# Two feature tiles of the FFN side by side, token combinations on VectorE, and weight parts issued later

## The chip, the cores and the metric

The kernel runs on one core of one Trainium2 chip. The metric is the device time of one execution in microseconds (us). Before the change the median of three runs is 2619.1 us (2618.94 to 2619.82).

## The reference

The program is a decoder trunk of two layers over 1040 tokens (16 meta tokens and 1024 inputs), model width 1024, all in float32:

```python
for l in range(DEPTH):
    h = rms_norm(h_res, attn_norm_g[l])
    z = h @ w_in[l]
    c_q, c_kv, k_pe, rq, rk, rv, rg = jnp.split(z, split_idx, axis=-1)
    y_mla = mla_mixer(c_q, c_kv, k_pe, ...)
    y_ret = retention_mixer(rq, rk, rv, rg, ...)
    y = jnp.concatenate([y_mla, y_ret], axis=-1) @ w_out[l]
    h_res = h_res + y
    hf = rms_norm(h_res, ffn_norm_g[l])
    gate, up = jnp.split(hf @ w_gate_up[l], 2, axis=-1)
    h_res = h_res + (jax.nn.silu(gate) * up) @ w_down[l]
return h_res[:, N_META:]
```

The change concerns the end of the output projection (`@ w_out`), the RMS norm behind it, and the gate and up projections of the FFN (width 2816).

## The kernel before, in words

**Precision and layout.** Activations lie transposed: features on the 128 partitions, tokens along the free dimension. Every float32 product is made of three matmuls (`mm3`, lines 312 to 317): each operand is split into a rounded high part and the remainder (`hi` and `lo`), and hi*hi (L315), hi*lo (L316) and lo*hi (L317) are summed in a PSUM bank. ScalarE makes a high part by a copy (L273 for FFN weights, L1173 for activations), VectorE the remainder by a subtraction (L275, L1174). So each operand costs one ScalarE and one VectorE instruction before TensorE can use it.

**The FFN in two token halves.** `HALVES` cuts the tokens of a layer into two halves j = 0 and 1 of H tokens: 520 in layer 0, where each half is worked on in two pieces (`subs`) of 260 columns, and 512 in one piece in layer 1. Gate and up weights of a feature tile f (128 rows of the 2816, 22 tiles) and the two halves of tokens, each cut into model features k = 0 to 3 and 4 to 7, form a 2x2 block product, computed with seven products instead of eight. The table `XK` gives for each product p its token operand (of eight feature tiles, four k-steps each) and its weight part:

- p = 1 uses B11 and p = 2 uses B21: the normalised first token half, k = 0 to 3 and 4 to 7;
- p = 5 uses T1, p = 6 T2, p = 7 T3 and p = 4 T4: differences of normalised tiles (the token combinations), T1 = half 1 minus half 0 for k < 4, T2 = half 1 for k + 4 minus T1, T3 = half 1 for k + 4 minus half 1 for k, T4 = half 0 for k + 4 minus T2;
- p = 3 uses B22: half 1, k = 4 to 7.

A product is 4 x 3 matmuls per piece, so a feature tile is 168 matmuls of 260 columns in layer 0 and 84 of 512 columns in layer 1. The products of a tile are summed into PSUM: X (p = 1, 6, 7, 4), Z (p = 2) and Y (p = 5, 3), and each is read out by ScalarE or VectorE behind it (L1285 to L1301). In layer 0 the two pieces of X of an odd tile f lie in one tile of two banks, `P0`; all else lies in tiles of one bank (`bank()`, six of them).

**Order at the start of the FFN.** The output projection runs over j and m (eight feature tiles of 128, L1187 to L1201): 24 matmuls a piece, added to the residual on VectorE (L1194), written to `hmid` (L1197), squared by ScalarE and summed into `ss` by GpSimd (L382). During j = 1 the generator `first_half` normalises half 0 and makes B11 and B21 beside it. Half 1 can be normalised only when all of j = 1 is done. `gate_up(0, ...)` therefore runs p = 1 and 2 first, and `second_half(6)` (L1319) then makes the factor of half 1: column sums of `ss` on TensorE (L1148), a chain of short VectorE instructions (`rsqrt`, L341 to L346), a spread by transposes (L1158, L1162) and two copies by ScalarE (L1159, L1163). Then come the normalised tiles (L1167, VectorE), T1 and T3 and T4 (L1331, L1338, L1345, on GpSimd) and T2 (L1333, VectorE), each split by L1173 and L1174. Tiles f = 1 to 21 follow with all operands ready, each in the order 1, 2, 6, 5, 7, 3, 4.

**Weights.** A tile's gate and up weights arrive as two raw tiles of 512 KB (`wload`, L232, three `raw` buffers, all on SyncE's queue, in a fixed order of units). `gu_weights_steps` (L1216) makes four parts of them: gate, two combinations (`s21`, `s34`; L1225 to L1231, VectorE) and half of up; each part is a `hi` and a `lo` tile, of which there are four buffers each. `gate_up` takes two steps for the next tile behind each product.

**The order of instructions** on an engine isn't the source's: a scheduler of the framework reorders the emitted program, as the quoted orders below show. Each engine then works through its own list in order and waits on semaphores.

Of the kernel before, what the change touches and what calls it, by code (L numbers as in the profile page):

```python
# [15 lines left out]
ALU = mybir.AluOpType  # L16
# [24 lines left out]
def units():  # L41
# [14 lines left out]
    for l in range(DEPTH):  # L56
# [22 lines left out]
        for _ in range(2):  # L79
            for m in range(8):  # L80
                add(f"out{m}", 1024, lambda a, l=l, m=m: rows(a["w_out"][l], 128 * m, 128)[:, [4, 5, 6, 7, 0, 1, 2, 3]])

        def gu(f, l=l):
            add(f"g{f}", 1024, lambda a, l=l, f=f: rows(a["w_gate_up"][l], 128 * f, 128))
            add(f"u{f}", 1024, lambda a, l=l, f=f: rows(a["w_gate_up"][l], FF + 128 * f, 128))

# [5 lines left out]
        for f in range(NF):  # L92
            gu(f)
# [81 lines left out]
def trunk(ctx: ExitStack, tc: tile.TileContext, xT, wts, gains, rope, cst, mask, outT):  # L175
# [49 lines left out]
    def wload():  # L225
# [5 lines left out]
        t = wp.tile([128, 1024], F32, tag="raw", name="raw", bufs=3)  # L231
# [324 lines left out]
    def layer(l, xs, ss):  # L556
# [585 lines left out]
        def half_sums(j):  # L1142
# [3 lines left out]
            ps = bank()  # L1146
# [7 lines left out]
        def half_spread(R, j):  # L1154
            a0 = b0 + H * j
            ps = bank()
# [28 lines left out]
        side_x = first_half()  # L1185
        for j in range(2):
            for m in range(8):  # L1187
                if j or m > 1:
                    ow[m] = weight(f"out{m}")
                for s0, n in subs:  # L1190
                    c0 = b0 + H * j + s0
                    early = j == 0 and m < 2
                    ps = dense(ow[m], 0, 128, ally, (c0, n, ()), first[m, s0] if early else None, k0=7 if early else 0)
                    V.tensor_tensor(out=h[m][:, c0:c0 + n], in0=ps, in1=h[m][:, c0:c0 + n], op=ALU.add)  # L1194
                    ahead()
                c0 = b0 + H * j
                SP.dma_start(out=hmid[128 * m:128 * m + 128, c0:c0 + H], in_=h[m][:, c0:c0 + H])  # L1197
                squares(h[m], ss, m, (c0, H, ()))
                if j:
                    for _ in range(1 if m < 6 else 2):  # L1200
                        next(side_x, None)  # L1201
        for _ in side_x:
            pass
        for a, b in ally:
            give(a, b)
# [5 lines left out]
        gw = {}  # L1211
# [27 lines left out]

        acts = {}  # L1240
# [20 lines left out]
        def gate_up(f, order, between):  # L1261
            prep = gu_weights_steps(f + 1) if f + 1 < NF else iter(())
            ez, act = slot("ez"), slot("act")
            X, Y, Z = {}, {}, {}
            if len(subs) > 1 and f % 2:
                P0 = pp.tile([128, 1024], F32, tag="P0", name="P0")
                X = {s0: P0[:, 512 * i:512 * i + 512] for i, (s0, _) in enumerate(subs)}

            def product(p, s0, n):
                name, wi, col = XK[p]  # L1270
                wh, wl = gw[f][wi]
                if p == 1 and s0 not in X:
                    X[s0] = bank()
                if p == 2:
                    Z[s0] = bank()
                if p == 5:
                    Y[s0] = bank()
                ps = (Z if p == 2 else Y if p in (5, 3) else X)[s0][:, :n]
# [152 lines left out]
```

## Time and profile before

| | |
|---|---|
| median of three runs | 2619.1 us |
| the profiled execution | 2621.88 us |
| its span, first to last instruction | 2620.1 us |
| TensorE busy | 2549.6 us (97%) |
| VectorE busy | 1423.2 us (54%) |
| ScalarE busy | 919.0 us (35%) |
| GpSimd busy | 476.9 us (18%) |
| mean granted TensorE clock | 0.987 of full speed |
| FFN's gate and up projections | about 613 to 1055 us (layer 0), 1919 to 2370 us (layer 1) |

PE is TensorE, PEld its weight load, DVE VectorE, ACT ScalarE, POOL GpSimd, SP SyncE. A stretch of time is counted from the start of the span. Matmuls overlap in the trace, so a busy PE may still be slow: the number of matmuls in a stretch tells more. "<-" in brackets names what ended an idle time.

### The profile page before, as it was taken

To read this page: it belongs to the slowest core of one execution; us is meant where nothing else is said; L and a number is where in the kernel's file an instruction comes from. 1 tells how busy PE (TensorE), PEld (TensorE's weight loads), DVE (VectorE), ACT (ScalarE), POOL (GpSimd) and SP (SyncE) were. 2 spreads that over 40 slices of the span, in tenths; PEclk is the share of its full clock that TensorE was granted. 3 is DMA by queue.
4 is the path that set the end of the run, shared out by engine and by line. 5 is a ranking of instruction groups with operands and counts; after the bars stand their busy time and mean duration, and the time that the engine had idled before them with its cause. 6 is when DMAs were issued, how large, how long until landed. Compare 5 with 4: busy or idle time off the path is not lost.

```text
span 2620.1 us, 39532 instructions
## 1 busy us (share of the span) xinstructions
PE 2549.6 (97%) x15962; PEld 2332.9 (89%) x15962; DVE 1423.2 (54%) x2719; ACT 919.0 (35%) x1830; POOL 476.9 (18%) x413
## 2 busy tenths in 40 slices
PE   7999999998999999999999999999989999999999
PEld 7999988897999999999998989988858888887887
DVE  7344676657644445654473436666585544546432
ACT  4231455534333333421141314565343333333210
POOL 3111442224111111000041113432241000100000
PEclk8999999998999999999999999999989999999999
DMA  4111011231222222522221110112312222225311
GB/s 162 41 66 41 29 45 34 82 132 55 74 85 73 78 82 74 215 96 79 74 98 49 58 49 29 37 29 94 133 52 97 73 89 81 73 104 202 112 41 65
DMA packets 63399, 208.35 MB, mean 80 GB/s; under 512 B 7153, under 2 KB 11377, under 8 KB 63217
## 3 DMA queue, kind: packets, MB, share of 16 engines
q1 hardware_dynamic: 63216, 205.84, 22.5%
q8 instruction: 125, 2.05, 0.3%
q14 instruction: 58, 0.47, 0.1%
HBM read 163.54 MB, written 42.27 MB: 79 GB/s over the span
## 4 chain that ended last, share of the span: by engine, by line
PE 54%; DVE 3%; issue 1%; ACT 1%; POOL 0%; DMA 0%; POOLq 0%; DVEq 0%; ACTq 0%
PE bank L315 16%; PE bank L317 16%; PE bank L316 16%; PE bank L1020 1%; PE bank L360 1%; PE bank L995 1%; DVE s L1174 0%; DVE s L1167 0%; PE P L494 0%; PE P L315 0%; PE bank L471 0%; PE P L498 0%; PE P L496 0%; PE P L316 0%; PE P L317 0%
## 5 line engine op out<-in xcount | busy, mean ns | idle before, releaser
L315 PE MATMUL bank<-s,hi 128*128 128x512 f32 (+4 forms) x3608 | 1213.8, 337 | 23.7 <-ACT s L1173 14.1
L316 PE MATMUL bank<-s,hi 128*128 128x512 f32 (+4 forms) x3608 | 1209.7, 335 | 7.5 <-DVE s L1174 4.8
L317 PE MATMUL bank<-s,lo 128*128 128x512 f32 (+4 forms) x3608 | 1205.7, 335 | 0.2 <-DVE lo L275 0.2
L315 PEld LDWEIGHTS bank<-s,hi 128*128 128x128 f32 x3608 | 681.0, 189 | 84.8 <-ACT s L1173 18.7
L316 PEld LDWEIGHTS bank<-s,hi 128*128 128x128 f32 x3608 | 682.4, 189 | 67.6 <-DVE s L1174 9.2
L317 PEld LDWEIGHTS bank<-s,lo 128*128 128x128 f32 x3608 | 682.0, 189 | 53.1 <-DVE lo L275 0.5
L244 ACT ACTIVATE hi<-raw 128x1024 fp32r<-128x1024 f32 (+1 forms) x132 | 134.5, 1019 | 521.1 <-PE bank L316 408.1
L1380 DVE TENSOR_TENSOR s<-bank,s 128x512 f32<-128x512 f32 (+3 forms) x240 | 139.8, 586 | 223.2 <-PE bank L317 222.3
L1301 POOL TENSOR_TENSOR s<-s,s 128x260 f32<-128x260 f32 (+1 forms) x66 | 87.2, 1321 | 770.5 <-ACT s L1297 449.5
L245 DVE TENSOR_TENSOR lo<-raw,hi 128x1024 fp32r<-128x1024 f32 (+1 forms) x132 | 157.7, 1195 | 121.9 <-ACT hi L244 121.3
L273 ACT ACTIVATE hi<-s 128x1024 fp32r<-128x1024 f32 x88 | 93.3, 1061 | 171.5 <-PE bank L316 164.9
L382 POOL TENSOR_TENSOR s<-s,t 128x520 f32<-128x520 f32 (+4 forms) x49 | 73.2, 1498 | 367.3 <-ACT t L378 345.4
L315 PE MATMUL P<-s,hi 128*128 128x260 f32 (+2 forms) x400 | 121.4, 304 | 4.6 <-DVE s L1294 3.0
L275 DVE TENSOR_TENSOR lo<-s,hi 128x1024 fp32r<-128x1024 f32 x88 | 108.1, 1229 | 30.2 <-ACT hi L273 29.6
L1287 DVE TENSOR_TENSOR s<-bank,s 128x260 f32<-128x260 f32 (+1 forms) x66 | 34.1, 516 | 160.5 <-PE bank L317 160.5
L317 PE MATMUL P<-s,lo 128*128 128x260 f32 (+2 forms) x400 | 116.8, 292 | 2.4 <-DVE lo L275 2.4
L273 ACT ACTIVATE hi<-raw 128x1024 fp32r<-128x1024 f32 x88 | 74.5, 846 | 124.3 <-issue 65.3
L316 PE MATMUL P<-s,hi 128*128 128x260 f32 (+2 forms) x400 | 116.5, 291 | 0.0
L554 POOL TENSOR_TENSOR s<-t 128x400 f32<-128x400 f32 (+3 forms) x50 | 61.1, 1223 | 264.3 <-DVE t L553 264.3
L1225 DVE TENSOR_TENSOR s<-raw 128x512 f32<-128x512 f32 x44 | 31.5, 716 | 127.9 <-DMA raw<-in_w 127.7
L315 PE MATMUL bank<-hi,s 128*128 128x256 f32 (+1 forms) x324 | 98.0, 303 | 0.7 <-ACT s L412 0.5
L317 PE MATMUL bank<-hi,s 128*128 128x256 f32 (+1 forms) x324 | 96.6, 298 | 0.0
(280 smaller groups left out, 3496.9 us busy)
## 6 DMA issues: line engine op xcount, KB each, us to landing
raw<-in_w SPq DMA_DIRECT2D x212, 512.0 KB, 3.4
hidden<-s SPq DMA_DIRECT2D x20, 520.0 KB, 2.9
s<-hidden SPq DMA_DIRECT2D x20, 520.0 KB, 5.4
hidden<-s SPq DMA_DIRECT2D x20, 512.0 KB, 2.9
s<-hidden SPq DMA_DIRECT2D x20, 512.0 KB, 5.2
s<-in_rope SPq DMA_DIRECT2D x8, 520.0 KB, 4.2
s<-in_x SPq DMA_DIRECT2D x8, 520.0 KB, 5.3
hmid<-s SPq DMA_DIRECT2D x16, 260.0 KB, 2.0
```

The lines of the kernel that those rows point to most:

```text
L244: A.activation(out=hi[:, :n], in_=t[:, :n], func=AF.Copy)
L245: V.tensor_tensor(out=lo[:, :n], in0=t[:, :n], in1=hi[:, :n].bitcast(F32), op=ALU.subtract)
L273: A.activation(out=hi[:, :n], in_=src, func=AF.Copy)
L275: V.tensor_tensor(out=lo[:, :n], in0=src, in1=hi[:, :n].bitcast(F32), op=ALU.subtract)
L315: PE.matmul(out, lhsT=lh, rhs=rh, start=start and i == 0, stop=False, skip_group_check=onto)
L316: PE.matmul(out, lhsT=lh, rhs=rl, start=False, stop=False, skip_group_check=onto)
L317: PE.matmul(out, lhsT=ll, rhs=rh, start=False, stop=stop and i == n - 1, skip_group_check=onto)
L382: e2.tensor_tensor(out=ss[:, c0:c0 + n], in0=ss[:, c0:c0 + n], in1=sq, op=ALU.add)
L554: G.tensor_tensor(out=out, in0=u[:p1], in1=v[:p1], op=ALU.add)
L1287: V.tensor_tensor(out=e1, in0=ps, in1=e1, op=ALU.add)
L1301: G.tensor_tensor(out=a2, in0=a2, in1=e2, op=ALU.mult)
L1380: V.tensor_tensor(out=h[m][:, c0:c0 + n], in0=ps, in1=h[m][:, c0:c0 + n], op=ALU.add)
```

## The change

Line numbers of the changed kernel differ by up to 60 (`mm3` is L318 to L320 there, splits are L1174 and L1175, weight splits L276 and L278). It does the following.

1. **Tiles 0 and 1 side by side** (`Job`, j0 and j1): each product is made for tile 0 and then for tile 1, in the order p = 1, 2, 5, 6, 7, 3, 4, so that p = 1 and 2 of both tiles stand ahead of the first token combination. PSUM for both at once: j0 has six banks, j1 uses `P0` for X and j0's Z for both Z and Y.
2. **Token combinations on VectorE**, in the order in which the products use them: T1, T2, T3, (B22,) T4. GpSimd makes none any more.
3. **The column sums of half 1** are issued after the first piece of tile 0's p = 2 and the transposes after tile 1's p = 1; both use bank Y. The last square of each half is added to `ss` by VectorE instead of GpSimd.
4. **Weights earlier for tiles 0 and 1**: their units stand behind `out5` and `out7` of j = 1 in the load order, the first three steps of each are taken during the output projection, there are four `raw` buffers instead of three, and one more load is issued at the start of the program, ahead of the input's second and third chunk of columns.
5. **From tile 2 on** `Job.both` issues a product's matmuls of both pieces and only then both read-outs (before: piece by piece), and the next tile's weight steps are taken 0, 2, 1, 2, 1, 2, 3 behind the seven products (before: two behind each).

The diff, cut:

```diff
-        for _ in range(2):
-            for m in range(8):
-                add(f"out{m}", 1024, ...)
...
+        for j in range(2):
+            for m in range(8):
+                add(f"out{m}", 1024, ...)
+                if j and m in (5, 7):
+                    gu((m - 5) // 2)
...
-        t = wp.tile([128, 1024], F32, tag="raw", name="raw", bufs=3)
+        t = wp.tile([128, 1024], F32, tag="raw", name="raw", bufs=4)
...
             SP.dma_start(out=cs, in_=cst)
+            wload()
             wload()
             wload()
...
+        def take(i, n):
+            for _ in range(n):
+                next(gw_steps[i], None)
...
+                if j and m == 7:
+                    gw_steps[1] = gu_weights_steps(1)
+                    take(1, 3)
...
-                squares(h[m], ss, m, (c0, H, ()))
+                squares(h[m], ss, m, (c0, H, ()), e2=V if m == 7 else G)
                 if j:
-                    for _ in range(1 if m < 6 else 2):
+                    for _ in range(1 if m < 2 else 2):
                         next(side_x, None)
+                if j and m == 5:
+                    gw_steps[0] = gu_weights_steps(0)
+                    take(0, 3)
+                    ahead()
...
+            def both(self, p, only=None):
+                self.mm(p, only)
+                if only is None or only == len(subs) - 1:
+                    self.ev(p)
...
-            for p in order:
-                between(p)
-                for s0, n in subs:
-                    product(p, s0, n)
...
-                for _ in range(2):
-                    next(prep, None)
...
+        j0 = Job(0)
+        j0.X, j0.Z, j0.Y = ([bank() for _ in subs] for _ in range(3))
+        P0 = pp.tile([128, 1024], F32, tag="P0", name="P0")
+        j1 = Job(1, [P0[:, 0:512], P0[:, 512:1024]][:len(subs)], j0.Z, j0.Z)
+        j0.both(1)
+        j0.mm(2, 0)
+        R = half_sums(1, j0.Y[0])
+        for i in range(1, len(subs)):
+            j0.mm(2, i)
+        j0.ev(2)
+        j1.both(1)
+        half_spread(R, 1, j0.Y[0], j0.Y[-1])
+        give(ss)
+        take(0, 2)
+        j1.mm(2)
+        take(1, 2)
+        for k in range(4):
+            norm_x(k, 1)
+            V.tensor_tensor(out=hv(h[k], 0), in0=hv(h[k], 1), in1=hv(h[k], 0), op=ALU.subtract)
+            two("T1", hv(h[k], 0))
+        j1.ev(2)
+        j0.mm(5)
+        j1.mm(5)
+        for k in range(4):
+            norm_x(k + 4, 1)
+            V.tensor_tensor(out=hv(h[k], 0), in0=hv(h[k + 4], 1), in1=hv(h[k], 0), op=ALU.subtract)
+            two("T2", hv(h[k], 0))
...
+        for k in range(4):
+            V.tensor_tensor(out=hv(h[k], 1), in0=hv(h[k + 4], 1), in1=hv(h[k], 1), op=ALU.subtract)
+            two("T3", hv(h[k], 1))
+            V.tensor_tensor(out=hv(h[k + 4], 0), in0=hv(h[k + 4], 0), in1=hv(h[k], 0), op=ALU.subtract)
...
+        for k in range(4):
+            two("B22", hv(h[k + 4], 1))
...
+        for k in range(4):
+            two("T4", hv(h[k + 4], 0))
...
+            for p, n in ((1, 0), (2, 2), (6, 1), (5, 2), (7, 1), (3, 2), (4, 3)):
+                job.both(p)
                 if f == NF - 1:
                     give(*fx.pop(XK[p][0]))
+                else:
+                    take(f + 1, n)
+            job.finish()
```

Three places in the order of instructions show what moves. **VectorE, layer 0, from the end of the rsqrt chain of half 1 on** (rynf: the factor; s_18 and the like: token tiles and their splits). Before:

```order
L346 SCALAR_TENSOR_TENSOR rynf_6683<-rt_6684,rynf_6683 128x5
L1167 SCALAR_TENSOR_TENSOR s18_5499<-s18_5499,gn_78,s31_5516 128x520
L1167 SCALAR_TENSOR_TENSOR s0_5503<-s0_5503,gn_78,s31_5516 128x520
L1167 SCALAR_TENSOR_TENSOR s35_5500<-s35_5500,gn_78,s31_5516 128x520
L1174 TENSOR_TENSOR s8_6707<-s18_5499,s8_6707 128x520
L1167 SCALAR_TENSOR_TENSOR s27_5504<-s27_5504,gn_78,s31_5516 128x520
L1333 TENSOR_TENSOR s18_5499<-s0_5503,s18_5499 128x520
L1174 TENSOR_TENSOR s5_6717<-s35_5500,s5_6717 128x520
L1167 SCALAR_TENSOR_TENSOR s7_5501<-s7_5501,gn_78,s31_5516 128x520
```

and now:

```order
L278 TENSOR_TENSOR lo_6892<-s13_6888,hi_6891 128x1024
L1168 SCALAR_TENSOR_TENSOR s18_5501<-s18_5501,gn_78,s31_5518 128x520
L1168 SCALAR_TENSOR_TENSOR s35_5502<-s35_5502,gn_78,s31_5518 128x520
L1358 TENSOR_TENSOR s18_5501<-s18_5501 128x520
L1358 TENSOR_TENSOR s35_5502<-s35_5502 128x520
L1168 SCALAR_TENSOR_TENSOR s7_5503<-s7_5503,gn_78,s31_5518 128x520
L1175 TENSOR_TENSOR s4_6746<-s18_5501,s4_6746 128x520
L1175 TENSOR_TENSOR s5_6751<-s35_5502,s5_6751 128x520
L1358 TENSOR_TENSOR s7_5503<-s7_5503 128x520
L1168 SCALAR_TENSOR_TENSOR s33_5504<-s33_5504,gn_78,s31_5518 128x520
L1308 TENSOR_TENSOR s2_6604<-bank_6599,s2_6604 128x260
```

The subtraction L1358 that makes T1 now stands in VectorE's own list (it was GpSimd's L1331), k runs 0, 1, 2, 3 and the tiles k + 4 come behind, and one read-out of tile 1's p = 2 (L1308) stands among them.

**TensorE, layer 0, up to the first matmul on T1.** Before, T1 and T2 are first used by the rows with bank_6774 and bank_6788, 8 matmuls of tile 1 (P0) behind the transposes:

```order
L317 MATMUL P0_6943<-s9_6248,lo_6636 128x260
L315 MATMUL P0_6943<-s10_6314,hi_6635 128x260
L316 MATMUL P0_6943<-s10_6314,hi_6635 128x260
L317 MATMUL P0_6943<-s10_6314,lo_6636 128x260
L315 MATMUL P0_6943<-s11_6380,hi_6635 128x260
L316 MATMUL P0_6943<-s11_6380,hi_6635 128x260
L317 MATMUL P0_6943<-s11_6380,lo_6636 128x260
L315 MATMUL bank_6774<-s8_6707,hi_6586 128x260
L315 MATMUL bank_6788<-s8_6707,hi_6586 128x260
L315 MATMUL bank_6974<-s12_6446,hi_6635 128x260
```

and now (bank_6600: tile 1's p = 2; bank_6601 and bank_6602: tile 0's p = 5):

```order
L318 MATMUL bank_6600<-s21_6454,hi_6532 128x260
L319 MATMUL bank_6600<-s21_6454,hi_6532 128x260
L320 MATMUL bank_6600<-s21_6454,lo_6533 128x260
L318 MATMUL bank_6601<-s4_6746,hi_6712 128x260
L318 MATMUL bank_6602<-s4_6746,hi_6712 128x260
L319 MATMUL bank_6601<-s4_6746,hi_6712 128x260
L320 MATMUL bank_6601<-s4_6746,lo_6713 128x260
L318 MATMUL bank_6601<-s5_6751,hi_6712 128x260
```

All 96 matmuls of p = 1 and 2 of both tiles stand ahead of the first one on T1 (bank_6601), 24 of them behind the transposes.

**TensorE, layer 0, an odd tile in the steady part**, p = 6 in P0. Before, the switch from piece 0 to piece 1 of P0 has four matmuls of another product between:

```order
L317 MATMUL P0_7388<-s25_6741,lo_7231 128x260
L315 MATMUL bank_7485<-s8_6707,hi_7230 128x260
L316 MATMUL bank_7485<-s8_6707,hi_7230 128x260
L317 MATMUL bank_7485<-s8_6707,lo_7231 128x260
L315 MATMUL bank_7485<-s5_6717,hi_7230 128x260
L315 MATMUL P0_7388<-s4_6711,hi_7230 128x260
L316 MATMUL P0_7388<-s4_6711,hi_7230 128x260
```

and now the pieces follow each other:

```order
L319 MATMUL P0_7381<-s34_6835,hi_7279 128x260
L320 MATMUL P0_7381<-s34_6835,lo_7280 128x260
L318 MATMUL P0_7381<-s1_6818,hi_7279 128x260
L319 MATMUL P0_7381<-s1_6818,hi_7279 128x260
L320 MATMUL P0_7381<-s1_6818,lo_7280 128x260
L318 MATMUL P0_7381<-s26_6823,hi_7279 128x260
```

The 24 matmuls of both pieces now stand in one run, and the read-outs of P0 behind it.

## Rows read from the trace of the kernel before

**Rows 1.** Stretches of 20 us, layer 0: busy us (matmuls), then granted clock, DMA share, GB/s.

```profile
core 0: us, PE busy (x) PEld busy (x) DVE busy (x) ACT busy (x) POOL busy (x), PEclk, DMA share, GB/s
...
620.00:640.00 20.00, 13.22 (x62) 11.62 (x63) 17.51 (x21) 6.73 (x12) 12.63 (x8) 0.74 0.08 27
...
680.00:700.00 20.00, 20.00 (x169) 20.00 (x168) 10.36 (x17) 7.95 (x15) 2.22 (x2) 1.00 0.24 80
```

**Rows 2.** Waits of TensorE over the whole span: us in total, times, longest.

```profile
PE bank L315 <- ACT s L1173: 14.1, 9, 3.9
```

**Rows 3.** Instructions in time, read-outs of products, both layers: start, us, what, idle before.

```profile
615.25 0.39 ACT L1285 ACTIVATE s<-bank 128x260 f32<-128x260 f32 x1 [1.04 <-PE bank L317]
...
699.50 0.43 DVE L1300 TENSOR_TENSOR s<-bank,s 128x260 f32<-128x260 f32 x1 [0.29 <-PE bank L317]
...
704.16 0.43 DVE L1287 TENSOR_TENSOR s<-bank,s 128x260 f32<-128x260 f32 x1 [3.38 <-PE bank L317]
705.60 0.43 DVE L1287 TENSOR_TENSOR s<-bank,s 128x260 f32<-128x260 f32 x1 [1.01 <-PE bank L317]
...
1922.17 0.60 ACT L1285 ACTIVATE s<-bank 128x512 f32<-128x512 f32 x1 [1.26 <-PE bank L317]
...
1999.49 0.69 DVE L1300 TENSOR_TENSOR s<-bank,s 128x512 f32<-128x512 f32 x1 [0.64 <-PE bank L317]
```

**Rows 4.** Instructions in time, layer 0, VectorE and GpSimd behind the factor of half 1.

```profile
624.48 3.12 DVE L1167 SCALAR_TENSOR_TENSOR s<-s,gn,s 128x520 f32<-128x520 f32 x3 [2.17 <-ACT s L1163]
...
635.60 1.79 DVE L1333 TENSOR_TENSOR s<-s,s 128x520 f32<-128x520 f32 x1
...
641.41 0.69 DVE L1333 TENSOR_TENSOR s<-s,s 128x520 f32<-128x520 f32 x1
...
649.02 4.84 DVE L1174 TENSOR_TENSOR s<-s,s 128x520 fp32r<-128x520 f32 x6
...
635.14 1.69 POOL L1331 TENSOR_TENSOR s<-s 128x520 f32<-128x520 f32 x1 [0.64 <-DVE s L1167]
```

**Rows 5.** Instructions in time, layer 1: column sums, transposes, VectorE behind them.

```profile
1878.86 0.95 PE L1148 MATMUL bank<-onesc,s 128*128 128x1 f32 x8
1879.67 0.47 PE L315 MATMUL bank<-s,hi 128*128 128x512 f32 x1
...
1928.97 1.12 PE L1158 MATMUL bank<-cs,rynf 128*128 128x128 f32 x4 [3.29 <-DVE rynf L346]
...
1930.76 3.08 DVE L1167 SCALAR_TENSOR_TENSOR s<-s,gn,s 128x512 f32<-128x512 f32 x3 [1.84 <-ACT s L1159]
...
1957.45 3.09 DVE L1174 TENSOR_TENSOR s<-s,s 128x512 fp32r<-128x512 f32 x5
```

**Rows 6.** SyncE's queue in time: writes of finished feature tiles, both layers.

```profile
723.16 0.33 SPq L1316 DMA_DIRECT2D hidden<-s  x1
...
1054.57 0.33 SPq L1316 DMA_DIRECT2D hidden<-s  x1
...
2019.72 0.33 SPq L1316 DMA_DIRECT2D hidden<-s  x1
...
2331.35 0.33 SPq L1316 DMA_DIRECT2D hidden<-s  x1
```

**Rows 7.** Tile P (P0), 660 to 1060 us: who waited; then one such wait in time.

```profile
  PEld P L315: 7.6, 21
...
840.58 0.39 PE L315 MATMUL P<-s,hi 128*128 128x260 f32 x1 [1.49 <-DVE s L1294]
```

**Rows 8.** Stretches of 4 us amid the operand work of half 1, both layers (columns: Rows 1).

```profile
640.00:644.00 4.00, 2.23 (x10) 1.41 (x10) 4.00 (x4) 1.27 (x2) 2.69 (x3) 0.76 0.00 0
1948.00:1952.00 4.00, 2.43 (x11) 1.63 (x9) 4.00 (x4) 0.98 (x2) 3.64 (x3) 1.00 0.01 2
```

**Rows 9.** ScalarE at the program's start; DMA issues: KB each, median us to landing.

```profile
14.64 1.06 ACT L244 ACTIVATE hi<-raw 128x1024 fp32r<-128x1024 f32 x1 [0.29 <-DMA raw<-in_w]
...
raw<-in_w SPq DMA_DIRECT2D x212, 512.0 KB, 3.4
```

More of the change, by code (lines that the diff above doesn't have):

```diff
@@ L90, in down @@
                 add(f"d{f0}_{i}", 1024, lambda a, l=l, f0=f0, n=n, i=i, w=w: rows(a["w_down"][l], w * i, w, f0, f0 + n))
-        for f in range(NF):
+        for f in range(2, NF):
             gu(f)
@@ L1183, in first_half @@
                 yield
[L1185 to L1189, printed above, removed]
-                for s0, n in subs:
[L1191 to L1197, printed above, removed]
-                squares(h[m], ss, m, (c0, H, ()))
-                if j:
-                    for _ in range(1 if m < 6 else 2):
[L1201 to L1205, printed above, removed]
         XK = {1: ("B11", 0, 0), 2: ("B21", 0, 512), 6: ("T2", 1, 0), 5: ("T1", 1, 512), 7: ("T3", 2, 0),
               3: ("B22", 2, 512), 4: ("T4", 3, 0)}
-        gw = {}
+        gw, gw_steps = {}, {}
         def gu_weights_steps(f):
@@ L1238, in gu_weights_steps @@
             wload()
+        def take(i, n):
+            for _ in range(n):
+                next(gw_steps[i], None)
+        side_x = first_half()
+        for j in range(2):
+            for m in range(8):
+                if j or m > 1:
+                    ow[m] = weight(f"out{m}")
+                if j and m == 7:
+                    gw_steps[1] = gu_weights_steps(1)
+                    take(1, 3)
+                for s0, n in subs:
+                    c0 = b0 + H * j + s0
+                    early = j == 0 and m < 2
+                    ps = dense(ow[m], 0, 128, ally, (c0, n, ()), first[m, s0] if early else None, k0=7 if early else 0)
+                    V.tensor_tensor(out=h[m][:, c0:c0 + n], in0=ps, in1=h[m][:, c0:c0 + n], op=ALU.add)
+                    ahead()
+                c0 = b0 + H * j
+                SP.dma_start(out=hmid[128 * m:128 * m + 128, c0:c0 + H], in_=h[m][:, c0:c0 + H])
+                squares(h[m], ss, m, (c0, H, ()), e2=V if m == 7 else G)
+                if j:
+                    for _ in range(1 if m < 2 else 2):
+                        next(side_x, None)
+                if j and m == 5:
+                    gw_steps[0] = gu_weights_steps(0)
+                    take(0, 3)
+                    ahead()
+        for _ in side_x:
+            pass
+        for a, b in ally:
+            give(a, b)
         acts = {}
@@ new lines, in layer @@
+        take(1, 3)
+        j1.mm(7)
+        for k in range(4):
+            two("B22", hv(h[k + 4], 1))
+        j0.ev(7)
+        j0.mm(3)
+        take(0, 3)
+        j1.ev(7)
+        j1.mm(3)
+        for k in range(4):
+            two("T4", hv(h[k + 4], 0))
+            give(h[k + 4])
+        j0.ev(3)
+        take(1, 3)
+        j1.ev(3)
+        j0.both(4)
+        j0.finish()
+        gw_steps[2] = gu_weights_steps(2)
+        take(2, 3)
+        j1.both(4)
+        j1.finish()
+        take(2, 8)
@@ L1265, in gate_up @@
+        for f in range(2, NF):
+            X = None
             if len(subs) > 1 and f % 2:
                 P0 = pp.tile([128, 1024], F32, tag="P0", name="P0")
[L1267 to L1278, printed above, removed]
[L1279 to L1301 removed]
@@ L1349, in layer @@
-        for _ in gu_weights_steps(0):
-            pass
-        order = (1, 2, 6, 5, 7, 3, 4)
-        gate_up(0, order, second_half)
-        for f in range(1, NF):
-            gate_up(f, order, lambda p: None)
+                else:
+                    take(f + 1, n)
+            job.finish()
         h = [slot("h") for _ in range(8)]
```

150 lines of the change are left out of this document (77 added, 73 removed).

## The prediction

> **What bounds the kernel now.** I read the page first: TensorE is busy 97% of the span, so no time can be won where the other engines work beside it, only where TensorE is held up. The stretches of 20 us show where that is: an undisturbed one carries 169 matmuls of 260 columns, the one from 620 us carries 62 at a granted clock of 0.74 [rows 1]. That is the start of the FFN in layer 0, and layer 1 has the same hole. The list of waits names the cause: TensorE waits most often there for a split of L1173 [rows 2], that is for operands of token half 1, which can only be made once the output projection has ended. So the operand chain ends last: column sums, factor, normalised tile, combination, split.
>
> How much is lost, worked out from read-outs. One matmul costs 0.12 us in layer 0: the two read-outs of a product's pieces, 12 matmuls apart, start at 704.16 and 705.60 [rows 3]. In layer 1 it is 0.232 us: 16 tiles of 84 between two hidden writes, 311.64 us [rows 6]. The output projection ends (call that E) one product of tile 0 ahead of that product's last read-out: 615.25 - 24 x 0.12 = 612.4 in layer 0, 1922.17 - 12 x 0.232 = 1919.4 in layer 1 [rows 3]. Tiles 0 and 1 end one tile before the last read-out of tile 2: 699.50 - 168 x 0.12 = 679.3 and 1999.49 - 84 x 0.232 = 1980.0 [rows 3]. So both tiles take **66.9 us** behind E in layer 0 and **60.6** in layer 1. Their matmuls alone are 336 x 0.12 = 40.3 and 168 x 0.232 = 39.0; with 1.2 for sums and transposes, 25.4 and 20.4 us are lost.
>
> A part of it is VectorE's. From 624.48 to 653.9 us it has 27 instructions on whole halves and takes 29.4 us. The same kind starts every 0.60 us where GpSimd rests (5 splits in 3.09), but lasts 1.79 where GpSimd has a subtraction of 1.69 beside it, against 0.69 [rows 4, 5]. At 0.60 to 0.68 each, the 27 would take about 16.8; the 12.6 above that are some 1.05 for each of GpSimd's 12 combinations.
>
> **The start of the FFN, after.** The order puts 72 matmuls ahead of the transposes in layer 0 and 41 in layer 1. Sums take 0.95, and from the transposes to the first normalised tile it is 1.8 [rows 5]. So normalising starts at E + 72 x 0.12 + 0.95 + 1.8 = E + 11.4, and E + 41 x 0.232 + 2.75 = E + 12.2. Before it was 624.48 - 612.4 = 12.1 and 1930.76 - 1919.4 = 11.4 [rows 4, 5]: the start wins nothing. The rsqrt chain and its square by VectorE lie beside those matmuls.
>
> From there VectorE's own list sets the pace. The last thing of that stretch that TensorE needs is the low part of tile 1's weight combination s34, for p = 4. Ahead of it stand 8 normalisations at 0.68, some 32 subtractions (12 combinations that came from GpSimd, 20 low parts) at 0.60, two short read-outs of 0.34, and itself at 1.2: 5.4 + 19.2 + 0.7 + 1.2 = **26.5**; in layer 1 26.4. ScalarE's high parts alternate with them; for the places where VectorE stands waiting for one I take 1.5 (between 0 and 4: the longest such wait of TensorE before was 3.9 [rows 2]). Behind that low part come the rest of the matmuls, 103 x 0.12 = 12.4 and 51 x 0.232 = 11.8. Sum: 11.4 + 26.5 + 1.5 + 12.4 = **51.8**, and 12.2 + 26.4 + 1.5 + 11.8 = **51.9**. Against 66.9 and 60.6 that is 15.1 and 8.7: **23.8 us**. TensorE still loses some 10 us in each layer; late next is VectorE, no longer GpSimd.
>
> **Odd tiles in layer 0.** A pair of tiles takes 331.41 / 8 = 41.43 us between hidden writes [rows 6], its 336 matmuls 40.3: 1.1 lost. P0 as one tile of two banks is why: piece 1's matmuls wait until piece 0's read-out is through, as at 840.58 for 1.49 us [rows 7]. With both pieces in one run, the read-outs lie under the next product's 24 x 0.12 = 2.9 us. 10 odd tiles x 1.1 = 11; the weight load's own waits on P0 sum to 7.6 [rows 7]. At 20 / 169 = 0.118 a matmul [rows 1] a pair would lose 1.6, so 16. I take **10**, with 7.6 and 16 as ends. Layer 1 has one piece and no P0: nothing.
>
> **What costs.** One more weight load stands ahead of the input's second columns: 512 KB, landing in 3.4 us, its high part 1.06 on ScalarE [rows 9] and its low part like it. ScalarE and VectorE are needed by the input then; I take **-1** (ends 0 and -2.5). The granted clock sinks where TensorE is thinly fed (below): **-2** for both layers (ends 0 and -5).
>
> **At nothing.** Four raw buffers move no load back in SyncE's list; a unit only waits for a buffer that comes free one use earlier. The loads of tiles 0 and 1 stand ahead of the last output weights' uses, but were issued long before E. Tile 2's up load must wait for tile 0's last use of its raw tile, near E + 41, and lands 3.4 later; its first user on VectorE stands near E + 48. Behind that waiting load on SyncE are the loads of tile 3 and the hidden writes, none of which is due before E + 52; if it came 7 us later, tile 2 would begin late. The steps moved behind products make a part 1.06 + 1.23 = 2.3 us after its buffer's last use, five products or 14 us ahead of need. The last square's sum on VectorE (0.69) replaces a slower one on GpSimd, beside the first 36 matmuls.
>
> **Sum.** 23.8 + 10 - 1 - 2 = 30.8. The profiled execution took 2621.88, 2.8 above the median of the runs, so 2591.1 there and **2588** in the median. With all the good ends (1.5 of waits back in each layer, 16, 0, 0) the gain is 42.8; with all the bad ones (2 x 2.5 more wait, 7.6, -2.5, -5) 18.9. Not all fall together: 2580 to 2598 is the forecast's own range. A measurement of this kernel tells 0.2% (5.2 us) from no change.
>
> **Rivals.**
> *The clock falls.* Tiles 0 and 1 still have stretches in which TensorE gets a few matmuls and waits. Of two such stretches with 10 and 11 matmuls in 4 us, one had a clock of 0.76 and the other 1.00 [rows 8], so thin feeding lowers it sometimes: 1.00 is the 2.4 GHz level, and 0.76 a mix with 1.2. If it stands at 1.2 GHz when the last low part comes, the matmuls behind cost double: 12.4 and 11.8 more. Half of that gives 2600, all of it 2612. The Trainium skill, page "TensorE: Matmul & The Clock Gate", section "A second HAM failure mode: psum-queue depth-cycling", says that frequent short idle times between groups of matmuls make the clock swing and cost throughput between bursts; by that rule the side-by-side order, which spreads matmuls thinly up to the last operand, would fare worse than before. The trace agrees for layer 0 alone. Against: the idle time shrinks, and the 20 us behind the hole ran at 1.00. Chance 0.17.
>
> *P0's waits only move.* If the next odd tile's p = 1 still meets a read-out in P0, the 10 go: 2598. Against: a whole even tile lies between. Chance 0.08.
>
> *Slower: VectorE's long instructions are its own.* The 1.79 could come from dense issue with ScalarE's reads, not from GpSimd. Then the some 43 instructions on VectorE's list, now with 12 more, each cost 1.1 more: 47 a layer, 2619 + 94 - 31 = 2682. It turns slower from 31 / 1.1 = 28 long ones of 86 in both layers. Against: five splits at 0.60 in a row without GpSimd [rows 5], and 0.69 at 641.41 amid the dense part [rows 4]. The Trainium skill, page "SBUF — State Buffer", section "Who interferes with whom", says that an instruction of VectorE with two inputs in SBUF blocks and is blocked by a GpSimd instruction that reads there, and by nothing else. The trace agrees. Chance 0.03.
>
> *No change.* The operand chain is as long as before because ScalarE's high parts come late instead (each of 20 by 1.2 us), or tile 2 waits for weights. Then the 23.8 go, which gives 2612, and with the bad ends of the clock and of the program's start, 4.5 more, 2617. Against: ScalarE has only 7 to 8 us of work in 20 [rows 1]. Chance 0.06.
>
> **How the numbers follow.** Forecast 0.66, clock 0.17, P0 0.08, no change 0.06, slower 0.03. The likeliest gives 2588. The range takes the forecast's 2580 to 2598, P0's 2598 and about 0.1 of the clock's case: **2579 to 2605**; about 0.19 is left out (0.03 of the forecast, 0.07 of the clock's, 0.06, 0.03). Faster 0.92, same 0.05, slower 0.03.
>
> **What would show it.** Right: the first L1168 behind the factor at E + 11 to 12; VectorE's subtractions there at 0.69 with GpSimd idle; tile 1's last product at E + 52 in both layers; pairs of hidden writes in layer 0 40.3 apart; no wait of L318 on P0. Wrong: a mean clock well below 1.00 in the 15 us before E + 52, subtractions of 1.7 without GpSimd, or a hole ahead of tile 2 on `hi` or `raw`.

## The result and the profile after

The changed kernel takes **2583.43 us** (median of four runs, 2581.58 to 2584.43) against 2619.02 (2614.44 to 2619.82): 0.9867 of the time, 95% interval 0.985 to 0.9884. The forecast was 2588 with a range of 2579 to 2605. The span of the profiled execution went from 2620.1 to 2582.0 us, 38.1 less.

The two 20 us stretches of the first tiles in layer 0, and a later one, in the changed kernel (busy us and, in brackets, instructions of each engine, then granted clock, DMA share, GB/s):

```profile
620.00:640.00 20.00, 16.61 (x121) 14.91 (x120) 20.00 (x34) 10.82 (x23) 0.00 (x0) 1.00 0.01 1
640.00:660.00 20.00, 18.24 (x131) 17.24 (x130) 18.43 (x32) 9.73 (x17) 5.13 (x4) 0.91 0.29 99
...
680.00:700.00 20.00, 20.00 (x169) 20.00 (x169) 9.95 (x17) 7.27 (x14) 2.14 (x3) 1.00 0.23 80
```

TensorE now issues 121 matmuls where it issued 62 [rows 1]. VectorE is busy without a pause (20.00 us, 34 instructions for 21) and GpSimd does nothing there. TensorE's waits for low parts of token operands, in the kernel before, the partner of the row of 14.1 us for high parts [rows 2] (total, times, longest):

```profile
PE bank L316 <- DVE s L1174: 4.8, 8, 1.1
```

and both kinds in the changed kernel:

```profile
PE bank L319 <- DVE s L1175: 5.5, 11, 0.7
PE bank L318 <- ACT s L1174: 4.3, 6, 1.8
```

Together 18.9 us have become 9.8, all of it by the high parts. The waits on P0 by read-outs of VectorE have gone from the list. VectorE in time, layer 0: the first normalisation behind the factor, a few combinations, and the low part of tile 1's s34.

```profile
619.40 1.43 DVE L1168 SCALAR_TENSOR_TENSOR s<-s,gn,s 128x520 f32<-128x520 f32 x2 [0.99 <-ACT s L1164]
620.75 1.30 DVE L1358 TENSOR_TENSOR s<-s 128x520 f32<-128x520 f32 x2
...
630.88 1.29 DVE L1365 TENSOR_TENSOR s<-s,s 128x520 f32<-128x520 f32 x2
...
645.13 1.22 DVE L278 TENSOR_TENSOR lo<-s,hi 128x1024 fp32r<-128x1024 f32 x1
```

And the read-outs by which the stretch is measured, the last one of p = 1 of tile 0 and of tile 2, both layers (ScalarE; in layer 0 the second piece's):

```profile
611.26 0.39 ACT L1306 ACTIVATE s<-bank 128x260 f32<-128x260 f32 x1 [1.04 <-PE bank L320]
...
663.50 0.39 ACT L1306 ACTIVATE s<-bank 128x260 f32<-128x260 f32 x1 [0.85 <-PE bank L320]
...
1890.88 0.60 ACT L1306 ACTIVATE s<-bank 128x512 f32<-128x512 f32 x1 [0.86 <-PE bank L320]
...
1943.37 0.60 ACT L1306 ACTIVATE s<-bank 128x512 f32<-128x512 f32 x1 [0.27 <-PE bank L320]
```

Both read-outs lie the same number of matmuls behind their tile's start, so their distance is what tiles 0 and 1 take behind the end of the output projection (E). It is **52.2 us** in layer 0 and **52.5** in layer 1. The kernel before took 67.0 and 60.6 by the same measure.

The steady part of layer 0, hidden writes of tiles 3 and 19:

```profile
701.96 0.33 SPq L1333 DMA_DIRECT2D hidden<-s  x1
...
1023.15 0.33 SPq L1333 DMA_DIRECT2D hidden<-s  x1
```

8 pairs in 321.19 us are 40.15 a pair, for 41.43 before [rows 6].

Stage by stage the gain of 38.1 us is: E of layer 0 comes 4.0 earlier (608.4 for 612.4), tiles 0 and 1 of layer 0 give 14.8, the rest of layer 0 up to E of layer 1 12.5 (1888.1 for 1919.4 there, 31.3 in all), tiles 0 and 1 of layer 1 8.1, the tiles behind them 0.7, and the way from the last hidden write to the end costs 2.0 more.

### The profile page after: what moved, and what is told of

It reads as the page before. It is cut to its first block, busy times and chain, and to the rows that moved or that the text cites. A ratio compares the mean times of both kernels' runs of the same rounds, so it can differ in the third digit from the quotient of the medians.

```text
span 2582.0 us, 39490 instructions
## 1 busy us (share of the span) xinstructions
PE 2528.0 (98%) x15962; PEld 2321.1 (90%) x15962; DVE 1412.6 (55%) x2747; ACT 917.3 (36%) x1830; POOL 430.6 (17%) x385
## 3 DMA queue, kind: packets, MB, share of 16 engines
q1 hardware_dynamic: 63216, 205.84, 22.9%
## 4 chain that ended last, share of the span: by engine, by line
PE 89%; DVE 6%; issue 2%; ACT 2%; DMA 1%; POOL 0%; POOLq 0%; SPq 0%; DVEq 0%; ACTq 0%
PE bank L318 24%; PE bank L320 24%; PE bank L319 24%; PE P L318 2%; PE P L319 2%; PE P L320 2%; PE bank L1024 2%; PE bank L363 1%; PE bank L999 1%; PE P L498 1%; PE bank L475 1%; PE P L500 1%; PE P L502 1%; DVE s L1175 1%; DMA raw<-in_w 0%
## 5 line engine op out<-in xcount | busy, mean ns | idle before, releaser
L318 PE MATMUL bank<-s,hi 128*128 128x512 f32 (+4 forms) x3592 | 1205.2, 336 | 16.4 <-ACT s L391 9.5
L320 PE MATMUL bank<-s,lo 128*128 128x512 f32 (+4 forms) x3592 | 1198.9, 334 | 0.0
L318 PEld LDWEIGHTS bank<-s,hi 128*128 128x128 f32 x3592 | 676.9, 189 | 75.0 <-ACT s L391 9.8
L320 PEld LDWEIGHTS bank<-s,lo 128*128 128x128 f32 x3592 | 677.6, 189 | 51.5
L247 ACT ACTIVATE hi<-raw 128x1024 fp32r<-128x1024 f32 (+1 forms) x132 | 134.5, 1019 | 520.2 <-PE bank L319 419.6
L278 DVE TENSOR_TENSOR lo<-s,hi 128x1024 fp32r<-128x1024 f32 x88 | 107.7, 1224 | 113.6 <-ACT hi L276 113.5
L276 ACT ACTIVATE hi<-s 128x1024 fp32r<-128x1024 f32 x88 | 93.3, 1061 | 164.1 <-PE bank L319 156.3
L385 POOL TENSOR_TENSOR s<-s,t 128x520 f32<-128x520 f32 (+4 forms) x45 | 65.9, 1467 | 363.8 <-ACT t L381 342.0
L318 PE MATMUL P<-s,hi 128*128 128x260 f32 (+2 forms) x416 | 122.6, 295 | 0.0
L319 PE MATMUL P<-s,hi 128*128 128x260 f32 (+2 forms) x416 | 122.1, 294 | 0.0
L320 PE MATMUL P<-s,lo 128*128 128x260 f32 (+2 forms) x416 | 121.8, 293 | 0.0
L1308 DVE TENSOR_TENSOR s<-bank,s 128x260 f32<-128x260 f32 (+1 forms) x66 | 34.0, 515 | 151.2 <-PE bank L320 150.9
L276 ACT ACTIVATE hi<-raw 128x1024 fp32r<-128x1024 f32 (+1 forms) x88 | 74.4, 846 | 101.7 <-PE bank L319 50.3
L318 PE MATMUL bank<-hi,s 128*128 128x256 f32 (+1 forms) x324 | 98.0, 303 | 1.6 <-DVE t L557 0.9
L320 PE MATMUL bank<-hi,s 128*128 128x256 f32 (+1 forms) x324 | 96.5, 298 | 0.0
L319 PE MATMUL bank<-lo,s 128*128 128x256 f32 (+1 forms) x324 | 96.5, 298 | 0.0
```

The lines of the kernel that those rows point to most:

```text
L247: A.activation(out=hi[:, :n], in_=t[:, :n], func=AF.Copy)
L276: A.activation(out=hi[:, :n], in_=src, func=AF.Copy)
L278: V.tensor_tensor(out=lo[:, :n], in0=src, in1=hi[:, :n].bitcast(F32), op=ALU.subtract)
L318: PE.matmul(out, lhsT=lh, rhs=rh, start=start and i == 0, stop=False, skip_group_check=onto)
L319: PE.matmul(out, lhsT=lh, rhs=rl, start=False, stop=False, skip_group_check=onto)
L320: PE.matmul(out, lhsT=ll, rhs=rh, start=False, stop=stop and i == n - 1, skip_group_check=onto)
```

## The experiments

The same measures of every run, from its own profile, stand in one table. "Tiles 0, 1" is the distance of the read-outs above, "pair" the mean of 8 pairs of hidden writes in layer 0, "tail" the time from the last hidden write of layer 1 to the end of the span. A dash means not needed.

| run | median us | tiles 0, 1: layer 0 | layer 1 | pair | tail |
|---|---|---|---|---|---|
| before | 2619.0 | 67.0 | 60.6 | 41.43 | 288.8 |
| changed | 2583.4 | 52.2 | 52.5 | 40.15 | 290.8 |
| e1: read-outs piece by piece | 2592.5 | 50.7 | 53.6 | 41.20 | 289.3 |
| e2: combinations on GpSimd | 2597.5 | 60.8 | 57.9 | - | 289.5 |
| e3: tile 0, then tile 1 | 2586.9 | 53.3 | 53.9 | - | 290.7 |
| e4: load later | 2583.4 | 52.2 | 52.7 | - | 291.0 |
| b1: before, four raw buffers | 2617.9 | 67.2 | 60.7 | - | 291.1 |
| b2: before, all on VectorE | 2609.5 | 59.6 | 58.3 | - | 289.0 |
| e7: 8 more on VectorE | 2594.4 | 56.5 | 56.2 | - | 290.9 |
| e5: sum on GpSimd | 2582.6 | 52.2 | 52.2 | - | 289.3 |
| e6: weights late | 2585.4 | 50.7 | 52.8 | - | 290.8 |
| e8: last product on VectorE | 2579.2 | 50.7 | 52.1 | - | 287.6 |
| e10: e8 and earlier transposes | 2579.8 | 49.6 | 52.3 | - | 287.8 |
| e11: e10 and s34's sums early | 2576.2 | 48.4 | 49.1 | - | 287.7 |

**e1, read-outs piece by piece.**

```diff
-                job.both(p)
+                for i in range(len(subs)):
+                    job.mm(p, i)
+                    job.ev(p, i)
...
```

> The changed kernel, but from tile 2 on each piece's matmuls are followed by its own read-out, as before; all else stays, the new spacing of the weight steps too. Theory (P0's two pieces wait for each other's read-out): pairs of hidden writes in layer 0 go from 40.15 back to about 41.4 us, ten odd tiles cost 12 us, the time goes from 2583.4 to about 2595; layer 1 unchanged. Rival (the spacing of the weight steps 0, 2, 1, 2, 1, 2, 3 is what freed the odd tiles): pairs stay at 40.2, time within 2 us of 2583.4.

2592.46 us (2590.3 to 2598.52), 9 more than the change where 12 had been expected; the pair goes to 41.20. So 1.05 of the 1.28 us that a pair won come from the joined read-outs, 10.5 over ten odd tiles. The other 0.23 a pair belong to something else; the spacing of the weight steps is a candidate that was not tried alone. In e1's profile TensorE's weight loads wait for P0 again, 5.5 us in 26 waits between 660 and 1040 us; in the changed kernel the list has no such wait there. So about half of the 10.5 us is seen as waits on P0.

**e2, combinations on GpSimd.**

```diff
-            V.tensor_tensor(out=hv(h[k], 0), in0=hv(h[k], 1), in1=hv(h[k], 0), op=ALU.subtract)
+            G.tensor_tensor(out=hv(h[k], 0), in0=hv(h[k], 1), in1=hv(h[k], 0), op=ALU.subtract)
```

and the same for T3 and T4.

> The changed kernel with T1, T3 and T4 made by GpSimd again, side by side order kept. Theory (GpSimd's subtractions stretch VectorE's beside them, and VectorE's list sets the end): 12 GpSimd instructions bring back 12 x 1.05 us and take away 12 x 0.60, plus the longer way through GpSimd: tiles 0 and 1 end 5 to 10 us later in each layer, the time is 2594 to 2603, and VectorE's instructions of 0.69 us show 1.7 beside GpSimd. Rival (the matmuls of both tiles ahead of the first combination made the gain, whoever combines): 0 to 3 us more, 2583 to 2587.

2597.5 us (2595.26 to 2598.82), 14.1 more: 8.6 in layer 0 and 5.4 in layer 1. VectorE and GpSimd in time, in e2:

```profile
631.90 3.51 DVE L1365 TENSOR_TENSOR s<-s,s 128x520 f32<-128x520 f32 x2
```

```profile
631.45 3.41 POOL L1375 TENSOR_TENSOR s<-s,s 128x520 f32<-128x520 f32 x2 [2.21 <-DVE s L1168]
```

Two T2 subtractions on VectorE take 3.51 us beside two of GpSimd; the same two took 1.29 in the changed kernel (630.88 above), where GpSimd rests. That is the collision, seen with GpSimd at work and without. The theory holds. The rival (0 to 3 us) is out as it stands, but a part of it is left: with the combinations back on GpSimd, tiles 0 and 1 still take 6.2 and 2.7 us less than before the change, so 8.9 us come from the rest of the change (the new order with its PSUM places), whoever combines.

**e3, tile 0 whole, then tile 1.** The start is emitted as p = 1, 2, 5, 6, 7, 3, 4 of tile 0 and then `j1.both(1)` to `j1.both(4)`; combinations and PSUM places stay.

> The changed kernel with tile 0 emitted whole and tile 1 behind it; combinations on VectorE in the same order, same PSUM places. Theory (VectorE's list sets the end): whatever TensorE does meanwhile, tiles 0 and 1 end when VectorE's list is through and the matmuls behind it are done: 0 to 4 us more a layer, 2583 to 2591. Rival (the order of the products made the gain): tiles 0 and 1 take again some 61 to 67 us behind the output projection, 2600 or more.

2586.89 us (2583.48 to 2590.07): 1.1 and 1.4 us more. The scheduler moves tile 1's products between those of tile 0 by itself, in the PSUM places left to them (P0 for X, tile 0's Z again); in its order 17 of them stand ahead of layer 1's transposes either way, and 10 instead of 24 ahead of layer 0's. So the order in the source is worth some 2.5 to 4 us (3.5 in the medians; the clock did not fall in e3's layer 0), and e3 is no test of what tile 1's matmuls ahead of the first combination are worth. What the free PSUM places are worth was not tried apart.

**e4, the additional load behind the input.**

```diff
-            wload()
             mf = t_(128)
...
+    wload()
+
     def gcol(l, name, i=0):
```

> The changed kernel with the additional weight load of the program's start issued behind the input's third chunk of columns. The output projection of layer 0 ended 4.0 us earlier than before the change (608.4 against 612.4), where a loss of 1 had been put down. Theory (the additional load ahead of the input costs 0 to 2.5 us, and the 4 come from elsewhere): 2581 to 2584. Rival (the earlier weight load is what made those 4): 2586 to 2588, and the first matmuls lose what they had gained.

2583.4 us (2581.87 to 2586.77): nothing either way.

**b1, the kernel before with four raw buffers and the additional load.**

```diff
-        t = wp.tile([128, 1024], F32, tag="raw", name="raw", bufs=3)
+        t = wp.tile([128, 1024], F32, tag="raw", name="raw", bufs=4)
...
+            wload()
             wload()
             wload()
```

> The kernel before, with four raw buffers and the additional weight load at the start, nothing else. Before, the profile has 108 matmuls in 40 to 60 us at a clock of 0.71; after, and in every variant of it with four raw buffers, 125 to 133 there. Theory (the deeper prefetch made the 4 us at the program's start that the sum had as a loss of 1): 2614 to 2616, and 125 or more matmuls in 40 to 60 us. Rival (that was the clock of one profile, or another part of the change): 2618 to 2620.

2617.94 us, ratio 0.9997 (0.9987 to 1.0006): no difference, although this profile has 126 matmuls in 40 to 60 us. The rival holds. E of layer 0 lies between 606.3 and 613.5 us over all profiles of this study, and in e10, whose order is the change's up to there, at 613.5. So the 4.0 us ahead of E lie inside the scatter of single profiles, and no run shows them to be the change's. Four raw buffers do not go with more matmuls there either: e6, e7 and e10, which have them, show 112 to 114 in 40 to 60 us.

**b2, the kernel before with all combinations on VectorE.**

```diff
-                    G.tensor_tensor(out=hv(h[k], 0), in0=hv(h[k], 1), in1=hv(h[k], 0), op=ALU.subtract)
+                    V.tensor_tensor(out=hv(h[k], 0), in0=hv(h[k], 1), in1=hv(h[k], 0), op=ALU.subtract)
```

and the same for T3 and T4.

> The kernel before, with T1, T3 and T4 on VectorE in the places where GpSimd had them; no side by side, old weight times. Theory (collisions with GpSimd stretched VectorE, and VectorE sets the end): per layer 12.6 us of collisions go and 7.2 of work comes, and the way through GpSimd gets shorter: 5 to 9 us a layer, 2601 to 2609. Rival (engine alone is worth nothing without the products' and combinations' order): 2615 to 2620.

2609.46 us (2608.97 to 2612.24), just outside what was expected: 7.4 us in layer 0, but only 2.3 in layer 1, where 5 to 9 had been put down. In layer 1 the long instructions have gone too, but VectorE now stands still for 2.50 us and 0.64 us until ScalarE has made a high part (at 1935.9 and 1942.6), and TensorE's last three waits there are for ScalarE. So the engine alone is 9.7 of the 22.9 us that the start won, the rest of the change without it (e2) is 8.9, and 4.3 come only from both together; taken out of the change, the engine costs 14.0.

**e7, eight more subtractions.**

```diff
+            for _ in range(2):
+                V.tensor_tensor(out=t_(520)[:, 0:H], in0=hv(h[k], 1), in1=hv(h[k], 0), op=ALU.subtract)
```

among the T1 steps, for k = 0 to 3.

> The changed kernel with 8 more subtractions of a token half on VectorE among the first combinations of each layer, whose results nobody uses. Theory (VectorE's list sets the end of tiles 0 and 1): 8 x 0.60 = 4.8 us later in each layer, 2583.4 + 9.6 = 2593. Rival (ScalarE's high parts or TensorE's products set it, VectorE has slack): under 4 us more in all, up to 2587.

2594.39 us (2588.57 to 2595.09): tiles 0 and 1 end 4.3 and 3.7 us later, for 4.8 of work on VectorE in each layer, and the median is 11.0 later. In layer 0 the changed kernel's profile has a fall of the clock that e7's has not (1.5 us, below); against the 50.7 of profiles without it, e7 is 5.8 later. TensorE's last wait of this stretch in layer 0 has moved by as much: it ends 36.3 us behind E in the changed kernel and 42.1 in e7.

```profile
644.66 0.55 PE L319 MATMUL bank<-s,hi 128*128 128x260 f32 x1 [0.47 <-DVE s L1175]
```

```profile
655.43 0.39 PE L319 MATMUL bank<-s,hi 128*128 128x260 f32 x1 [0.47 <-DVE s L1175]
```

Both wait for a low part of VectorE, and 120 matmuls follow in both. VectorE's list does set the end.

**e10, earlier transposes and the last product on VectorE.**

```diff
+        if len(subs) > 1:
+            j1.mm(1, 0)
+            half_spread(R, 1, j0.Y[0], j0.Y[-1])
+            j1.mm(1, 1)
+            j1.ev(1)
...
-                        G.tensor_tensor(out=a2, in0=a2, in1=e2, op=ALU.mult)
+                        (V if self.f == NF - 1 else G).tensor_tensor(out=a2, in0=a2, in1=e2, op=ALU.mult)
```

> The changed kernel with two edits more. First, in layer 0 the transposes stand between the two pieces of tile 1's p = 1 (60 matmuls ahead instead of 72): VectorE's list starts 12 x 0.12 = 1.4 us earlier, and by the theory tiles 0 and 1 end 1.4 us earlier; by the rival (the start is not what holds VectorE) nothing. Second, the last tile's last multiplication (p = 4 of tile 21) on VectorE instead of GpSimd, where it took 2.06 us in layer 1 with the first split of the down projection and TensorE waiting behind it: 1 to 2 us a layer by the theory, nothing if the load of hidden rows is what is waited for. Together 2579 to 2581; rival 2583.

2579.82 us (2579.61 to 2581.06). Layer 0's stretch is 49.6 us, 1.1 under the 50.7 of the profiles whose clock did not fall there (below). The median alone does not show the earlier transposes, since e8, without them, is no slower.

**e8, the last product alone** (the second half of that edit).

> The changed kernel with the multiplication behind p = 4 of tile 21 on VectorE instead of GpSimd, nothing else. From the last hidden write to the end the changed kernel took 290.8 us, the one before 288.8: GpSimd's instruction of 2.06 us, the split behind it and a clock that fell to 0.57 for 4 us. Theory (that instruction is on the path): 287.5 to 289.5 there, 1 to 2 us less in each layer, 2580 to 2582. Rival (ScalarE's split of the next weight between is what counts): 290.8 again, 2583.

2579.19 us (2578.56 to 2580.72), ratio 0.9845 to before. The tail is 287.6, less than in any run with GpSimd there (288.8 to 291.1). Of the 3.2 us against the changed kernel only some 1 to 2 belong to the edit: that profile has its clock at 0.79 for 8 us at the start of layer 1's down projection (2332 to 2340 us, 25 matmuls, 37 in e8), and the five runs with GpSimd whose clock stays at 1.00 there (before, b2, e1, e2, e5) have tails of 288.8 to 289.5. No gain is seen in layer 0. In the changed kernel, GpSimd and then ScalarE, at the end of the FFN of layer 1:

```profile
2329.46 2.06 POOL L1321 TENSOR_TENSOR s<-s,s 128x512 f32<-128x512 f32 x1 [19.04 <-issue]
...
2331.55 0.63 ACT L1258 ACTIVATE s<-s 128x512 fp32r<-128x512 f32 x1 [2.23 <-POOL s L1321]
...
2332.24 0.50 PE L318 MATMUL bank<-s,hi 128*128 128x512 f32 x1 [1.49 <-ACT s L1258]
```

and in e8 the same multiplication and split:

```profile
2330.37 0.68 DVE L1321 TENSOR_TENSOR s<-s,s 128x512 f32<-128x512 f32 x1
...
2331.08 1.23 ACT L1258 ACTIVATE s<-s 128x512 fp32r<-128x512 f32 x2 [0.75 <-DVE s L1321]
```

0.68 us on VectorE for 2.06 on GpSimd, which again had VectorE's two-input work beside it. This wait was in the kernel before, too; the change did not touch it.

**e5, the last square's sum on GpSimd** (`e2=G` for every m).

> The changed kernel with the last square of each half added by GpSimd, as before. Theory (this edit is worth nothing: the sum lies beside TensorE's first products, of which 36 of 0.12 us stand ahead of the column sums in layer 0): 2583 to 2585. Rival (GpSimd's slower sum delays the column sums and all behind them): 1 us or more in each layer, 2586 or more.

2582.61 us (2579.3 to 2584.07): nothing, as put down.

**e6, weights of tiles 0 and 1 late** (their units behind `out7`, both `take(i, 3)` behind the output projection's loop).

> The changed kernel with the weights of tiles 0 and 1 loaded behind those of the output projection and their first steps emitted behind it, as before. Theory (nothing at the start of the FFN waited for weights; the scheduler places these steps beside the output projection anyway): 2582 to 2586, tiles 0 and 1 still end 52 us behind the output projection. Rival (the earlier weights are what lets the products of both tiles stand ready): holes on hi or lo tiles behind the output projection, 2590 or more.

2585.44 us (2583.7 to 2587.52), tiles 0 and 1 at 50.7 and 52.8: nothing beyond the scatter. The scheduler puts the steps beside the output projection wherever they are written.

**e11, s34's sums ahead of the factor.**

```diff
-        take(0, 2)
+        take(0, 3)
         j1.mm(2)
-        take(1, 2)
+        take(1, 3)
...
         j1.mm(6)
-        take(0, 3)
+        take(0, 2)
...
         j0.mm(7)
-        take(1, 3)
+        take(1, 2)
```

on top of e10.

> The kernel with the earlier spread and the last product on VectorE, and one edit more: the two subtractions that make tile 1's weight combination s34 are issued before half 1's factor (VectorE has idle pieces there) and no longer late in the stretch among the token combinations. Theory (VectorE's list from the factor to tile 1's s34 sets the end): 2 x 0.60 = 1.2 us less in each layer, 2577 to 2578 against 2579.8. Rival (by then other splits or TensorE's own products end the stretch): no change, 2579 to 2581.

**2576.15 us** (2573.33 to 2577.97), ratio 0.9831 to before (0.9816 to 0.9846): the fastest version of this study. Layer 0's stretch is 1.2 shorter, as worked out; layer 1's 3.2. There the clock stayed at 1.00 through the whole stretch in this profile; in e10 it fell to 0.57 behind TensorE's last wait, which is some 1.1 of the 3.2. TensorE's last wait in layer 0 is now for the low part of s34 itself:

```profile
642.61 0.39 PE L320 MATMUL P<-s,lo 128*128 128x260 f32 x1 [0.39 <-DVE lo L278]
```

## Why the prediction was right

**What bounds.** Shown: TensorE waited at the start of the FFN for operands of half 1, and VectorE's list made them. e7 lengthens the list and the end follows; e11 shortens it and the end follows. e3 says little here, because TensorE got nearly the same order. b2 shows the limit: in its layer 1 VectorE waits 3.1 us for high parts of ScalarE, the cause that the rival of no change had named, and only 2.3 us are won.

**The sum for tiles 0 and 1.** Step by step, against what stands in the profile of after:

| step | layer 0: forecast | measured | layer 1: forecast | measured |
|---|---|---|---|---|
| E to the first normalisation | 11.4 | 619.40 - 608.4 = 11.0 | 12.2 | 11.5 |
| to the end of s34's low part, with waits | 28.0 | 646.35 - 619.40 = 26.9 | 27.9 | 27.5 |
| matmuls behind it | 12.4 | 660.6 - 646.35 = 14.3 | 11.8 | 13.5 |
| all | 51.8 | 52.2 | 51.9 | 52.5 |

The 1.5 us of waits were nearly all absent in layer 0, where VectorE never stopped from 619.40 to 640; in layer 1 they were 0.9. What came instead stands in the third step: 112 and 57 matmuls stood behind that low part, not 103 and 51, and the clock fell there (below). The gains forecast, 15.1 and 8.7, were 14.8 and 8.1.

That the step of 26.5 came out so well is in part luck. Of the 20 low parts counted in it, 14 stand ahead of s34's low part in layer 0 and 6 behind it; the list has in their place the four T2 subtractions and the two sums that make s34, which the forecast left out. So the 32 subtractions were right in number and not in kind. s34 serves p = 7 and p = 3, not p = 4 as the prediction has it, and its low part (646.35) was not quite the last thing that TensorE waited for: that was the token low part for which the wait shown under e7 ends at 644.66, and s34's is first used at 648.04. In e11 s34's low part is the last wait, as forecast. The mechanism holds by this, VectorE's list bounds the stretch, but the list's last item was named too late by 1.7 us.

**The collisions.** The stretching was read rightly as GpSimd's doing (the stretch has 26 instructions, not 27, which makes it 13.2 us instead of 12.6): with GpSimd idle every combination takes 0.6 to 0.7 us, and e2 brings the long ones back. The rival that made the long instructions VectorE's own is out. The Trainium skill, page "SBUF — State Buffer", section "Who interferes with whom", has this as an exclusive lock, taken between VectorE's instructions with two inputs in SBUF and GpSimd's that read there. The trace agrees: 3.51 us for two beside GpSimd and 1.29 alone.

**The odd tiles.** The mechanism held (e1), the size was low: the pair gained 1.28 us where 1.0 was taken, 12.8 in all for 10. The bound of 16 contains it. A pair's 336 matmuls now take 40.15, which is 0.1195 each and not the 0.12 of the sum, so the loss before was at least 1.28 and not 1.1. The rival that P0's waits only move is out, since none is left.

**The clock.** The rival was half right: the clock did fall in the thin stretch, but for a short time. The same 6 us, 35 to 41 us behind E of layer 0 (columns: stretch, TensorE busy and matmuls, granted clock, DMA share, GB/s), the changed kernel first:

```profile
643.40:649.40 6.00, 5.49 (x30) 0.72 0.27 87
```

and e8:

```profile
645.70:651.70 6.00, 5.45 (x43) 1.00 0.26 87
```

TensorE is busy as long in both, with 30 matmuls at 0.72 (a mix of the levels 1.2 and 2.4 GHz) and 43 at 1.00: 13 x 0.12 = 1.5 us, which is the difference between 52.2 and 50.7 in the table. The fall was short, as the next 6 us of the changed kernel show:

```profile
649.40:655.40 6.00, 6.00 (x52) 1.00 0.25 87
```

So most of the matmuls behind the last low part ran at full clock, and the rival's 12.4 us did not come. In the fall matmuls start 0.22 us apart instead of 0.12. It cost 1.5 us in layer 0 and some 1.1 in layer 1, near the allowance of 1 us a layer. The Trainium skill, page "TensorE: Matmul & The Clock Gate", section "A second HAM failure mode: psum-queue depth-cycling", says that frequent short idle times between groups of matmuls make the clock swing. The trace agrees in part: the clock fell in the changed kernel, e4 and e5 and did not in e1, e6 and e8, though TensorE has nearly the same idle times in all six (5.0 to 5.2 us behind E of layer 0). The thin stretch is the faster order here either way. The prediction saw the fall before the change in layer 0 alone; layer 1 of that trace has it too, at 0.50 with 3 matmuls from 1931.38 to 1935.38 us.

**The program's start.** Put down at -1; the profile showed +4.0, but b1 and e4 show no effect and the scatter of E hides one of this size. Neither the -1 nor the +4.0 is shown.

**At nothing.** The earlier weights (e6), the sum on VectorE (e5) and the load at the start (e4) cost and gave nothing that a measurement tells.

Together: the profiles differ by 38.1 us where 30.8 was forecast. The first tiles gave 22.9 for 23.8, with the clock's fall inside, for which 2 more had been put down; the rest of layer 0 gave 12.5 for 10; and the tiles behind in layer 1, 0.7 for nothing. The remaining +4.0 ahead of E (for -1) and -2.0 in the tail lie inside the scatter of single profiles; the tail's is the clock (e8). In the medians the change is 4.6 us better than 2588. So the terms with a mechanism came out within 3 us each, and part of the closeness of the whole is luck: too few matmuls behind the low part were made up for by waits that did not come.

## What to carry to other kernels

When an engine's instructions look slow in one stretch only, look at what its neighbour does in that stretch: moving 12 small instructions from GpSimd to a busier VectorE made VectorE's list shorter. The engine is not all of it: alone it was worth 9.7 of 22.9 us, and the new order without it 8.9. Where a chain of small instructions bounds a stretch, count that engine's list from the first input to the last output; everything that can be issued before the first input (here two weight subtractions) comes off the end. A scheduler that reorders makes the order in the source matter little (2.5 to 4 us here); that it needs places in PSUM which the program leaves free is argued and not shown.

## What was not expected of the hardware

The granted clock differs between executions of nearly the same instructions: in the stretch above it fell to 0.72 in the changed kernel, e4 and e5, and stayed at 1.00 in e1, e6 and e8. What decides it stays open. At the program's start 108 to 138 matmuls fit into 40 to 60 us, and the end of the first output projection scatters over 7 us. The tail scatters between 288.8 and 291.1 us with unchanged code, and here the clock is the difference: 288.8 to 289.5 where it stays at 1.00 at the start of layer 1's down projection, 290.7 to 291.1 where it falls to some 0.8. So a difference of a few us between the ends of two single profiles says nothing. The stage tables compare stretches instead, and even there one fall of the clock is worth 1.1 to 1.5 us.
